# A decoder layer in fp32 parts: the left factors of the fourth unit made early, four raw rooms, and a retuned modulation ring

## The chip, the cores and the metric

The kernel runs on one core of one Trainium2 chip. The metric is the device time of one execution in microseconds, as the median of several runs. The engines are named as in the profile: PE is TensorE (matmuls), PEld its weight loads, DVE is VectorE, ACT is ScalarE, POOL is GpSimd, SP the engine that issues most DMAs.

## The reference, cut to what matters

One decoder layer over 256 tokens of width 2048, all in float32. The layer has a mixer (three attention-like branches behind one wide input projection, joined by `w_out`) and a SwiGLU feed-forward part. Both are modulated by a vector `c`:

```python
mod = jax.nn.silu(c) @ w_ada[l] + b_ada[l]            # 2048 -> 6 x 2048
shift1, scale1, gate1, shift2, scale2, gate2 = jnp.split(mod[:, None, :], N_MOD, axis=-1)
h = rms_norm(x, norm1_gain[l]) * (1 + scale1) + shift1
x = x + gate1 * mixing_sublayer(h, w_in[l], ...)      # ends in y @ w_out
h = rms_norm(x, norm2_gain[l]) * (1 + scale2) + shift2
x = x + gate2 * swiglu(h, w_ffn_in[l], w_ffn_out[l])  # (silu(gate) * up) @ w_ffn_out, width 5632
```

## The kernel before, in words

**Products.** Every float32 weight tile is split into a high and a low part of type float32r: ScalarE casts (`whi`), VectorE subtracts (`wlo`). The left factors (activations, transposed) are split in the same way. `mm3` makes each product from three matmuls: high by high, high by low, low by high (lines 169 to 172). The weights come from HBM in transfers of 512 KB, each into a *raw room*, and are split into a *weight room* (`whi` and `wlo`). In `load_weights` there are four of each. A raw room is free again when the low part has been made; a weight room when TensorE has used it.

**Stages.** The input projection with the three branches; the gates and branch projections (`gate_block`, `y_block`); `w_out` in four column blocks of 512, the last with its weights held for both halves of the tokens; then the eleven units of the feed-forward part, each 512 columns of `gate` and of `up`; then `w_ffn_out` in two output passes of two column blocks each (`fast_products` over `OUT_A`, then over `OUT_B`), the second with a remainder.

**Fast units.** Units 2 to 10 (`FAST`) and both output passes go through `fast_products`. It walks over pairs of 128-row chunks. A *plain* pair is multiplied directly: two column blocks, two halves of the tokens, two chunks, 24 matmuls. A *fast* pair uses seven products in place of eight (Winograd's form of Strassen's scheme), 21 matmuls. For it `load_pair` makes sums and differences of the raw weights on VectorE in two scratch tiles (`ta`, `tb`), and the left factors need sums too. After the last fast pair, four combinations (lines 1427 to 1430) and four additions (`merge`, line 1386) bring the shared products into the four accumulators; the first two additions are wanted by the unit's last pair.

**Left factors of the output passes.** `sums_of_unit(n)` makes the summed and split left factors for one unit of 512 activations, for fast pairs of the output passes. It uses the scratch tiles `AR0` and `A8`, the same that fast pairs of these passes use for `ta` and `tb`. Units 4, 5 and 6 are made at hooks of pairs 2, 4 and 6 of the first pass; the fourth one, unit 3, at the hook of its last pair, with its result in the tiles `OD` and `KD`. Until then `OD` and `KD` serve as two more raw rooms (`more_raws`), so that the first pass has six. Only the second pass uses unit 3's sums.

**Modulation in the background.** The columns of `w_ada` for the later modulations are fetched in steps of 512 KB into a ring of rooms (`ring["tags"]`, two to six of them) and multiplied and added on VectorE (`ada_mac`, line 297). A generator makes one step for each *tick*; each pair of chunks ticks `rate` times, so that a block of 16 chunks makes eight times its rate. `RATES_OP` are the rates of the first three `w_out` blocks, `RATES_FFN` those of the four passes of the first two feed-forward units, whose end flushes what is left; `RATE_OUT` is that of the output passes. `gate2` is made in two portions, 24 steps from the `w_out` stage on and 8 in the first output pass. A multiply-add is written when the ring is full, just before the load that reuses its room, and it is ordered behind the latest weight split of that point (`state["split"]`).

**What sets the order.** All is written once, without loops at run time. A planner puts the instructions of each engine in order: it simulates the program, and when an engine is free, it takes the ready instruction of the highest priority. Priority is program order; `prio()` moves what stands in it `AHEAD` = 4000 instructions forward. A tile with one buffer goes to the next user when the last one lets it go. Weight loads, splits and additions stand in `prio()`; `sums_of_unit` and `ada_mac` do not. On the chip each engine, and SP with its DMAs, goes through its own list in order and waits at each entry for what that entry needs.

Of the kernel before, what the change touches and what calls it, by code (L numbers as in the profile page):

```python
# [31 lines left out]
SEG_SHIFT1, SEG_SCALE1, SEG_GATE1, SEG_SHIFT2, SEG_SCALE2, SEG_GATE2 = range(6)  # L32
RATE_IN, RATE_MID = 0.8, 0.6

RATES_OP, RATES_FFN, RATE_OUT = (0.8, 0.5, 0.15), (0.75, 0.8, 0.6, 0.6), 0.5
GATE2_CUT = 12
LOOK = 3
DEFER = 4
AHEAD = 4000
# [38 lines left out]
def trunk(ctx: ExitStack, tc: tile.TileContext, I, out):  # L78
# [31 lines left out]
    @contextmanager  # L110
    def prio(offset=AHEAD):

        with tc.high_priority(offset=offset):
            start = tc.cur_priority
            yield
            n = tc.cur_priority - start
        tc.cur_priority += n

    state = {"rate": 0.0}
# [239 lines left out]
    ring = {"tags": ("AR0", "AR1"), "n": 0}  # L359
# [5 lines left out]
    macs = []  # L365
# [16 lines left out]
    def ada_segment_steps(acc, seg, done, zero=True, ks=range(KC)):  # L382


        for k in ks:
            for j in range(2):
                while len(macs) >= len(ring["tags"]):
                    mac()
                raw = araw([P, 2 * NB])
                c0 = seg * D + j * 2 * NB  # L390
                with prio():
                    nc.sync.dma_start(raw, w_ada[k * P : (k + 1) * P, c0 : c0 + 2 * NB])
                macs.append((acc, j, k, raw, done if (k, j) == (ks[-1], 1) else None, zero))
                yield
# [976 lines left out]
    def fast_products(src, c0, c1, order, at, sums, own, other, tags, hooks={}, more=False):  # L1371


        ws = []

        def load(n):
            while len(ws) < min(n, len(order)):
                ws.append(load_pair(src, order[len(ws)][0], c0, c1, order[len(ws)][1], tags))

        load(LOOK if hooks else len(order))  # L1380
        o = [[own([P, NB]) for _ in range(NT)] for _ in range(2)]
        shared = []
        end = len(order)
        first_fast, last_fast = (f(n for n, (_, fast) in enumerate(order) if fast) for f in (min, max))
        last_plain = max(n for n in range(last_fast) if not order[n][1])
        add = lambda dst, x: nc.vector.tensor_tensor(dst, dst, x, op=ALU.add)  # L1386

        def merge(half):
            with prio():
                add(o[0][half], (first, third)[half])  # L1390
                add(o[1][half], u[:, 1 - half])

        for n, (p, fast) in enumerate(order):
            tick(2 * state["rate"])
            if n in hooks:
                hooks[n]()
            load(n + LOOK)
            w = ws[n]
            if n == 1 and later:
                with tc.issue_after(state["mm"].ins), prio():  # L1400
                    later.pop()()
            for half in range(2):
                if n == last_fast + 2 + half:
                    merge(half)
            merged = n > last_fast
            if fast:
                if not shared:
                    shared = [other([P, NB]) for _ in range(4)]
                    p1, p5, p7, p6 = shared
                s = sums[p]  # L1410
                a, b = 2 * p, 2 * p + 1
                lefts = (at(a, 0), at(b, 0), s[3], s[0], s[2], s[1], at(b, 1))
                for dst, (h, l), (wh, wl) in zip((p1, o[0][0], o[1][0], p5, p7, p6, o[0][1]), lefts, w):
                    mm3(dst, h, l, wh, wl, n == first_fast and any(dst is x for x in shared), n == last_fast)
            else:
                for c in range(2):
                    for t in range(NT):
                        for k in range(2):
                            h, l = at(2 * p + k, t)

                            closed = n == end - 1 and not more or merged or (c, t) == (1, 1) and n == last_plain
                            mm3(o[c][t], h, l, *w[c][k], n == 0 and k == 0, k == 1 and closed, merged)
            if n == last_fast:
                with prio():
                    u, first, third = S("KC", [P, 2, NB]), S("T6", [P, NB]), scr([P, NB])
                    nc.scalar.copy(first, p1)
                    nc.vector.tensor_tensor(u[:, 0], p6, first, op=ALU.add)
                    nc.vector.tensor_tensor(u[:, 1], p5, u[:, 0], op=ALU.add)
                    nc.vector.tensor_tensor(third, p7, u[:, 0], op=ALU.add)
                    nc.vector.tensor_tensor(u[:, 0], p5, third, op=ALU.add)  # L1430
        for half in range(2):
            if end <= last_fast + 2 + half:
                merge(half)
        return o
# [76 lines left out]
    def sums_of_unit(n):  # L1511

        e = OUT_UNITS[n]
        full = S(OUT_TAGS[0], [P, 4, T])
        nc.vector.tensor_tensor(full, act[e][0].bitcast(F32), act[e][1].bitcast(F32), op=ALU.add)
        sf = S(OUT_TAGS[1], [P, 4, 2, P])
        sums_of(sf, [full[:, :, t * P : (t + 1) * P] for t in range(NT)], slice(0, 4, 2), slice(1, 4, 2))
        hi, lo = (S(tag, [P, 4, 2, P], F32R) for tag in (("H2", "H3"), ("H4", "H5"), ("H6", "H7"), ("OD", "KD"))[n])
        nc.scalar.copy(hi, sf)
        nc.vector.tensor_tensor(lo, sf, hi.bitcast(F32), op=ALU.subtract)  # L1520
        for m in range(2):
            out_sums[2 * e + m] = [(hi[:, j, m, :], lo[:, j, m, :]) for j in range(4)]


    state["more_rooms"] = ()
    state["more_raws"] = ("OD", "KD")
    state["chain"] = None
    hooks = {at: (lambda n=n: sums_of_unit(n)) for n, at in enumerate((2, 4, 6))}
    state["rate"] = RATE_OUT
    ring["tags"] = ("OS1", "OS2")  # L1530
    bg.append(gate2_end())
# [9 lines left out]
    def rows_of_gate2(j):  # L1541
        for c in (slice(0, NB), slice(NB, 2 * NB)):
            ps = misc_bank([P, NB])
            with tc.issue_after(state["mm"].ins):
                for i, x in enumerate(parts[j]):
                    nc.tensor.matmul(ps, ones_r, x[:, c], start=i == 0, stop=i == 1)
            nc.scalar.copy(state["gate2"][j][:, c], ps)
# [7 lines left out]
    behind = 1 + max(n for n, (_, fast) in enumerate(OUT_A) if fast)  # L1555
    assert behind + 2 < len(OUT_A)
    hooks[behind] = lambda: parts_of_gate2(0)
    hooks[behind + 1] = lambda: both(0)
    hooks[behind + 2] = lambda: (rows_of_gate2(1), sums_of_unit(3))
    o = fast_products(w_fo, 0, NB, OUT_A, act_at, out_sums, acc_bank, misc_bank, OUT_TAGS, hooks)  # L1560
    gate2 = [a[:, c : c + NB] for a in state["gate2"] for c in (0, NB)]
    with prio():
        for n in range(2):
            for t in range(NT):
                add_out(n, t, o[n][t])
    state["more_raws"] = ()
    o = fast_products(w_fo, 2 * NB, 3 * NB, OUT_B, act_at, out_sums, misc_bank, acc_bank, OUT_TAGS, more=True)
    for n in (2, 3):
        bring_back(n, f"H{n}")
# [6 lines left out]
    n, pss = 3, o[1]  # L1576
# [42 lines left out]
```

## Time and profile before

| | before |
|---|---|
| median of 3 runs | 1586.41 us (1585.59 to 1587.01) |
| profiled execution, its own time | 1587.38 us |
| its span, first to last instruction | 1585.6 us |
| busy: PE, PEld | 1572.5 us, 1299.3 us |
| busy: DVE, ACT, POOL | 1347.2 us, 860.8 us, 12.4 us |
| moved by DMA | 402.26 MB, mean 254 GB/s |
| granted TensorE clock | 1.000 |

The profile is of one execution, so a time taken from it stands against 1587.38 us, and a median against 1586.41 us. A busy PE is not PE at its peak, because matmuls are pipelined and their ends are modelled; the time between the starts of matmuls, and the busy time of the weight loads in a stretch of fixed length, tell more.

### The profile page before, as it was taken

Reading aid. Unit: us, or ns where it says so; the run is one execution under the profiler, and the core shown is the slowest. Engines: PE = TensorE matmul, PEld = TensorE weight load, DVE = VectorE, ACT = ScalarE, POOL = GpSimd, SP = SyncE. Lnnn points to the kernel's source line nnn. Section 1 sums busy time; section 2 is a strip of 40 time slices with the busy share of each in tenths; the row PEclk is TensorE's granted clock in tenths of the full one; section 3 lists DMA queues with packets and bytes.
Section 4 is the critical chain, followed back from the end, with each engine's and each line's share of the span. In section 5 each row is a group of like instructions: output and inputs, shape, how many; then the busy total and the mean of one; then the engine's idle time right before and its main releaser. Section 6 shows DMA issues by size and latency. Waiting matters only on the chain.

```text
span 1585.6 us, 20226 instructions
## 1 busy us (share of the span) xinstructions
PE 1572.5 (99%) x7219; PEld 1299.3 (82%) x7219; DVE 1347.2 (85%) x1642; ACT 860.8 (54%) x1198; POOL 12.4 (1%) x24
## 2 busy tenths in 40 slices
PE   8999999999999999999999999999999999999998
PEld 7878888888888878888887888888888888888887
DVE  6889996888888686977877887999999998999986
ACT  5654448875765444444444645555555555455553
POOL 1000000000000000000000000000000000000000
PEclk9999999999999999999999999999999999999999
DMA  9999997677788889988888685666666666876664
GB/s 328 361 325 322 335 302 240 222 226 230 230 269 270 302 299 311 318 277 298 293 276 301 210 282 188 212 205 194 199 200 206 196 197 226 290 238 192 223 209 147
DMA packets 196316, 402.26 MB, mean 254 GB/s; under 512 B 13102, under 2 KB 28116, under 8 KB 196216
## 3 DMA queue, kind: packets, MB, share of 16 engines
q1 hardware_dynamic: 194952, 397.75, 76.2%
q0 software_dynamic: 1088, 3.16, 0.5%
q8 instruction: 57, 0.93, 0.2%
q14 instruction: 43, 0.35, 0.1%
q10 hardware_dynamic: 176, 0.07, 0.0%
HBM read 395.68 MB, written 5.24 MB: 253 GB/s over the span
## 4 chain that ended last, share of the span: by engine, by line
PE 88%; DVE 4%; DMA 3%; ACT 3%; issue 2%; POOL 0%; SPq 0%; ACTq 0%; DVEq 0%; POOLq 0%
PE acc L172 21%; PE acc L171 21%; PE acc L170 21%; PE misc L171 6%; PE misc L170 6%; PE misc L172 6%; ACT whi L162 1%; DVE wlo L163 1%; DMA raw<-w_br_gla 1%; PE acc L451 1%; PE misc L820 1%; DMA raw<-w_out 1%; PE misc L1130 1%; DVE wlo L1338 1%; PE misc L444 0%
## 5 line engine op out<-in xcount | busy, mean ns | idle before, releaser
L162 ACT CAST whi<-raw 128x1024 fp32r<-128x1024 f32 x325 | 329.4, 1018 | 352.6 <-PE acc L172 226.6
L163 DVE TENSOR_TENSOR wlo<-raw,whi 128x1024 fp32r<-128x1024 f32 x325 | 380.2, 1178 | 146.5 <-ACT whi L162 144.4
L170 PE MATMUL acc<-whi,H 128*128 128x512 f32 x1145 | 447.3, 392 | 1.1 <-ACT H L463 0.8
L171 PE MATMUL acc<-wlo,H 128*128 128x512 f32 x1145 | 446.9, 390 | 0.8 <-DVE wlo L163 0.7
L172 PE MATMUL acc<-whi,H 128*128 128x512 f32 x1145 | 446.4, 390 | 0.4 <-DVE H L470 0.4
L170 PEld LDWEIGHTS acc<-whi,H 128*128 128x128 f32 x1145 | 214.9, 188 | 45.7 <-ACT H L463 1.3
L172 PEld LDWEIGHTS acc<-whi,H 128*128 128x128 f32 x1145 | 214.8, 188 | 45.8 <-DVE H L470 1.6
L171 PEld LDWEIGHTS acc<-wlo,H 128*128 128x128 f32 x1145 | 215.1, 188 | 44.8 <-DVE wlo L163 1.7
L1352 ACT CAST whi<-raw 128x1024 fp32r<-128x1024 f32 (+1 forms) x163 | 155.4, 968 | 111.8 <-PE acc L172 35.1
L1338 DVE TENSOR_TENSOR wlo<-raw,whi 128x1024 fp32r<-128x1024 f32 (+1 forms) x163 | 177.9, 1114 | 11.1 <-ACT whi L1352 9.8
L172 PE MATMUL acc<-whi,A 128*128 128x512 f32 x234 | 91.1, 390 | 0.0
L171 PE MATMUL acc<-wlo,A 128*128 128x512 f32 x224 | 87.4, 390 | 1.2 <-DVE wlo L163 1.2
L170 PE MATMUL acc<-whi,A 128*128 128x512 f32 x224 | 87.9, 392 | 0.0
L170 PE MATMUL misc<-whi,H 128*128 128x512 f32 (+1 forms) x201 | 78.2, 389 | 0.9 <-DVE misc L1386 0.9
L171 PE MATMUL misc<-wlo,H 128*128 128x512 f32 (+1 forms) x201 | 78.1, 389 | 0.0
L172 PE MATMUL misc<-whi,H 128*128 128x512 f32 (+1 forms) x201 | 77.8, 387 | 0.0
L1338 DVE TENSOR_TENSOR A<-raw,A 128x1024 fp32r<-128x1024 f32 (+2 forms) x59 | 61.2, 1048 | 4.6 <-ACT A L1352 4.2
L1352 ACT CAST A<-raw 128x1024 fp32r<-128x1024 f32 (+1 forms) x47 | 45.9, 989 | 33.4 <-PE acc L172 11.6
L297 DVE SCALAR_TENSOR_TENSOR ada<-AR,csil,ada 128x1024 f32<-128x1024 f32 x39 | 49.4, 1278 | 3.4 <-DMA AR<-w_ada 3.4
L172 PEld LDWEIGHTS acc<-whi,A 128*128 128x128 f32 x234 | 43.9, 188 | 9.1
L171 PEld LDWEIGHTS acc<-wlo,A 128*128 128x128 f32 x224 | 42.1, 188 | 10.4 <-DVE wlo L163 1.9
L170 PEld LDWEIGHTS acc<-whi,A 128*128 128x128 f32 x224 | 42.1, 188 | 9.0 <-ACT whi L162 0.5
(502 smaller groups left out, 2494.7 us busy)
## 6 DMA issues: line engine op xcount, KB each, us to landing
raw<-w_in SPq DMA_DIRECT2D x205, 512.0 KB, 5.1
raw<-w_ffn_in SPq DMA_DIRECT2D x176, 512.0 KB, 4.6
raw<-w_ffn_out SPq DMA_DIRECT2D x74, 512.0 KB, 5.1
AR<-w_ada SPq DMA_DIRECT2D x58, 512.0 KB, 5.0
raw<-w_out SPq DMA_DIRECT2D x32, 512.0 KB, 5.5
OS<-w_ada SPq DMA_DIRECT2D x24, 512.0 KB, 6.1
KC<-w_ada SPq DMA_DIRECT2D x24, 512.0 KB, 5.4
KD<-w_ada SPq DMA_DIRECT2D x21, 512.0 KB, 5.4
```

What stands on the lines that cost most here:

```text
L162: state["cast"] = nc.scalar.copy(hi[:, :n, :], raw[:, :n, :])
L163: state["split"] = nc.vector.tensor_tensor(lo[:, :n, :], raw[:, :n, :], hi[:, :n, :].bitcast(F32), op=ALU.subtract)
L170: nc.tensor.matmul(ps, lh, rh, start=start, stop=False, skip_group_check=seeded)
L171: nc.tensor.matmul(ps, lh, rl, start=False, stop=False, skip_group_check=seeded)
L172: state["mm"] = nc.tensor.matmul(ps, ll, rh, start=False, stop=stop, skip_group_check=seeded)
L297: nc.vector.scalar_tensor_tensor(acc, raw, c, acc, op0=ALU.mult, op1=ALU.add)
L451: state["warm"] = nc.tensor.matmul(ps, ones_r, wide, start=True, stop=True)
L820: nc.tensor.matmul(ps[:n, t * N_GLA + h, :].rearrange("p (s l) -> p s l", l=L), at(f, h, t)[:, :n], odd(at(f, h, t)), start=True, stop=True,)
L1130: nc.tensor.transpose(ps[:, i, :], src[:, i * P : (i + 1) * P], ident)
L1338: done = nc.vector.tensor_tensor(dst, x, y, op=ALU.subtract)
L1352: nc.scalar.copy(hi[:, :n, :], src)
```

## The change

- The rates of the background steps: fewer in the second and third `w_out` blocks, more in two passes of the first two feed-forward units.
- The ring: where it has more than three rooms, a multiply-add is written one step earlier, so that its room is given up a step before the load that reuses it is written.
- The combinations and additions of a unit (`soon`): in the feed-forward units they are moved 8000 instructions forward instead of 4000. The two output passes keep 4000.
- `sums_of_unit(3)` moves from the last pair of the first output pass to pair 8.
- `OD` and `KD` are no raw rooms any more, so the first output pass has four, as the second one has.

```diff
-RATES_OP, RATES_FFN, RATE_OUT = (0.8, 0.5, 0.15), (0.75, 0.8, 0.6, 0.6), 0.5
+RATES_OP, RATES_FFN, RATE_OUT = (0.8, 0.3, 0.0), (0.75, 0.9, 0.7, 0.6), 0.5
...
-                while len(macs) >= len(ring["tags"]):
+                while len(macs) >= len(ring["tags"]) - (len(ring["tags"]) > 3):
                     mac()
...
+        soon = AHEAD if hooks or more else 2 * AHEAD
         load(LOOK if hooks else len(order))
...
         def merge(half):
-            with prio():
+            with prio(soon):
                 add(o[0][half], (first, third)[half])
                 add(o[1][half], u[:, 1 - half])
...
             if n == last_fast:
-                with prio():
+                with prio(soon):
                     u, first, third = S("KC", [P, 2, NB]), S("T6", [P, NB]), scr([P, NB])
...
     state["more_rooms"] = ()
-    state["more_raws"] = ("OD", "KD")
     state["chain"] = None
-    hooks = {at: (lambda n=n: sums_of_unit(n)) for n, at in enumerate((2, 4, 6))}
+    hooks = {at: (lambda n=n: sums_of_unit(n)) for n, at in enumerate((2, 4, 6, 8))}
...
-    hooks[behind + 2] = lambda: (rows_of_gate2(1), sums_of_unit(3))
+    hooks[behind + 2] = lambda: rows_of_gate2(1)
     o = fast_products(w_fo, 0, NB, OUT_A, act_at, out_sums, acc_bank, misc_bank, OUT_TAGS, hooks)
...
-    state["more_raws"] = ()
     o = fast_products(w_fo, 2 * NB, 3 * NB, OUT_B, act_at, out_sums, misc_bank, acc_bank, OUT_TAGS, more=True)
```

## The prediction

> **What bounds the kernel now.** I read the page first, then the stretches of 20 us, then the chain of waits, and last the engines' timelines around each stretch that falls short.
>
> ```profile
> span 1585.6 us, 20226 instructions
> PE 1572.5 (99%) x7219; PEld 1299.3 (82%) x7219; DVE 1347.2 (85%) x1642; ACT 860.8 (54%) x1198; POOL 12.4 (1%) x24
> ```
>
> TensorE is the bound. The profiled execution took 1587.38 us, 1.8 us more than its span and 0.97 us more than the median of 1586.41. No edit removes a matmul, so the change can only win what TensorE now waits, or add waits.
>
> ```profile
> 560.00:580.00 20.00, 19.19 (x84) 15.35 (x83) 15.37 (x17) 7.36 (x7) 0.00 (x0) 1.00 0.87 300
> 840.00:860.00 20.00, 19.44 (x84) 15.12 (x83) 18.11 (x18) 9.57 (x12) 0.53 (x1) 1.00 0.88 291
> 1340.00:1360.00 20.00, 19.08 (x89) 15.56 (x88) 18.48 (x26) 10.95 (x13) 0.00 (x0) 1.00 0.95 347
> 1460.00:1480.00 20.00, 19.70 (x87) 15.61 (x85) 19.57 (x28) 10.41 (x14) 0.00 (x0) 1.00 0.51 169
> 1500.00:1520.00 20.00, 20.00 (x90) 16.57 (x89) 17.60 (x21) 11.23 (x12) 0.00 (x0) 1.00 0.77 239
> 960.00:1300.00 340.00, 340.00 (x1533) 282.15 (x1533) 315.11 (x381) 192.08 (x215) 0.09 (x1) 1.00 0.63 200
> ```
>
> After each stretch and its length stand the busy times of TensorE, its weight loads, VectorE, ScalarE and GpSimd with their counts, the granted clock, the DMA share and GB/s. A full stretch holds 16.57 us of weight loads (1500:1520), so what is missing measures the loss: (16.57-15.35)/16.57x20 = 1.5 us in the first row, 1.75 in the second, 1.2 in the third. In the fourth, part of what is missing is smaller matmuls, so I measure it by starts below. The granted clock is 1.00 throughout. The 340 us of fast units lose nothing. Hence the stock that this change can draw on is about 5 us, of which the stretch at 560 lies in a stage that only the ring edit reaches.
>
> ```profile
> 575.00 0.50 PE L171 MATMUL acc<-wlo,A 128*128 128x512 f32 x1 [0.76 <-DVE wlo L163]
> 853.29 0.39 PE L170 MATMUL acc<-whi,A 128*128 128x512 f32 x1
> 854.09 0.50 PE L171 MATMUL acc<-wlo,A 128*128 128x512 f32 x1 [0.41 <-DVE wlo L163]
> 1340.62 0.39 PE L170 MATMUL misc<-whi,H 128*128 128x512 f32 x1
> 1340.85 0.39 PE L171 MATMUL misc<-wlo,H 128*128 128x512 f32 x1
> ...
> 1343.11 0.39 PE L172 MATMUL misc<-whi,H 128*128 128x512 f32 x1
> 1344.42 0.47 PE L170 MATMUL misc<-whi,H 128*128 128x512 f32 x1 [0.92 <-DVE misc L1386]
> 1479.09 0.61 PE L170 MATMUL acc<-whi,H 128*128 128x512 f32 x2
> 1480.00 0.50 PE L170 MATMUL acc<-whi,H 128*128 128x512 f32 x1 [0.30 <-ACT whi L1352]
> ```
>
> Matmuls of 512 columns start 0.23 us apart (1340.62, 1340.85). From 1343.11 to 1344.42 is 1.31, a stall of 1.1. The pair at 1479.09 puts its second start at 1479.32; to 1480.00 is 0.68, a stall of 0.45, and with the slower restart about 0.55. The waits named are the additions (L1386), a cast and twice a split.
>
> **Part 1, additions of the fast units at twice the priority.**
>
> ```profile
> 1334.44 3.49 DVE L1338 TENSOR_TENSOR wlo<-raw,whi 128x1024 fp32r<-128x1024 f32 x3
> 1337.85 0.68 DVE L1427 TENSOR_TENSOR KC<-acc,T 128x512 f32<-128x512 f32 x1
> ...
> 1341.84 1.23 DVE L1338 TENSOR_TENSOR wlo<-raw,whi 128x1024 fp32r<-128x1024 f32 x1 [1.52 <-ACT whi L1352]
> 1342.98 0.69 DVE L1430 TENSOR_TENSOR KC<-acc,scr 128x512 f32<-128x512 f32 x1
> 1343.58 0.69 DVE L1386 TENSOR_TENSOR misc<-misc,KC 128x512 f32<-128x512 f32 x1
> 1340.76 1.05 ACT L1352 CAST whi<-raw 128x1024 fp32r<-128x1024 f32 x1 [4.29 <-DMA raw<-w_ffn_out]
> ```
>
> In the last fast unit the first combination (L1427) sits behind three splits of 1.16, and the last one (L1430) behind a split whose cast waited 4.29 us for the first weights of the output pass. VectorE then stands idle 1.52 us although L1430's input is ready. With the doubled offset the four combinations and first two additions (6 x 0.60 to 0.69 = 3.9) go ahead of at least two of the three splits: they run from about 1335.6 and end about 1339.5, where TensorE wants the last of them at 1343.34. The 1.1 us go, with the slow restart 1.2. Late next are the displaced splits: the second would end at 1340.8, just when TensorE reads it (1340.85), so up to 0.3 could come back. The other eight fast units have the same code, but the 340 us row shows no loss there; the split that the additions can overtake belongs to the unit's last pair, which TensorE reads some 5 us later. I book 0, with a bound of 0.6 for one late split. Total -1.2 (from -1.2 to +0.6; not lower, as no more is lost there).
>
> **Part 2, the fourth unit's left factors moved from the last pair of the first output pass to its pair 8.**
>
> ```profile
> 1471.47 1.22 DVE L1515 TENSOR_TENSOR AR<-A,A 128x1024 f32<-128x1024 f32 x1
> 1472.72 0.76 DVE L1306 TENSOR_TENSOR A<-AR 128x256 f32<-128x256 f32 x2
> 1473.85 0.42 DVE L1306 TENSOR_TENSOR A<-AR,A 128x256 f32<-128x256 f32 x1
> 1476.12 1.22 DVE L1520 TENSOR_TENSOR KD<-A,OD 128x1024 fp32r<-128x1024 f32 x1
> 1474.31 1.05 ACT L1519 CAST OD<-A 128x1024 fp32r<-128x1024 f32 x1 [1.87 <-DVE A L1306]
> 1478.90 1.05 ACT L1352 CAST whi<-A 128x1024 fp32r<-128x1024 f32 x1 [2.13 <-DVE A L1338]
> ```
>
> Removed here: 1.22, four short sums from 1472.72 to 1474.27 (1.55) and 1.22, together 4.0 us of VectorE, and 1.05 of ScalarE, all right before the first fast pair of the second output pass, which needs the same scratch tiles AR0 and A8. The cast at 1478.90 waited 2.13 us for that pair's last difference, and TensorE at 1480.00 waits for the cast. Without the 4.0 us the 0.55 stall goes. No DMA moves with it. It is added where three sister units already run without a stall, ahead of their hook because their inputs are long there; VectorE stands idle in that place:
>
> ```profile
> 1376.70 1.23 DVE L1338 TENSOR_TENSOR wlo<-raw,whi 128x1024 fp32r<-128x1024 f32 x1 [1.22 <-ACT whi L1352]
> ```
>
> Splits there wait for casts, and casts for TensorE to free a weight room, so VectorE has such gaps, and a plain pair lets a split be some 5 us late; the 4.0 fit in. If instead the planner lets pair 8 take AR0 and A8 first, the 4.0 and the cast's 1.05 stand before pair 10, which needs the same tiles and whose splits are wanted at once, and TensorE could lose as much: +5.1 at most. I take 0, by the three sisters. Total -0.55 (from -0.55 to +4.5).
>
> **Part 3, four raw rooms instead of six in the first output pass.** Per plain pair TensorE works 24 x 0.227 = 5.44 us on two transfers of 512 KB, so four rooms turn over in 10.9 us. A turn costs the landing, a cast (1.05) and a split (1.23).
>
> ```profile
> raw<-w_ffn_out SPq DMA_DIRECT2D x74, 512.0 KB, 5.1
> DMA to landing us min/median/max: 4.5/7.4/10.0
> ```
>
> The first row is the page's median over all. The second is the raw tiles' own answer for 1331 to 1345, when six loads, two of gate2 and two of the modulation are in flight together. By the first a turn is 7.4, by the worst 12.3. The second output pass is the same loop with four rooms and loses nothing (1500:1520), so I book 0; fewer loads in flight at 1335 even help. Bounds 0 and, below as a rival, +15.
> [...]
>
> **Part 4, rates.** A block of 16 chunks ticks eight times. In the first three `w_out` blocks the steps fall from 8x(0.8+0.5+0.15) = 11.6 to 8x(0.8+0.3) = 8.8; in the first two FFN units they rise from 22 to 23.6, and 15 instead of 12 steps fall there.
>
> ```profile
> 840.81 1.28 DVE L297 SCALAR_TENSOR_TENSOR T<-A,csil,T 128x1024 f32<-128x1024 f32 x1
> ...
> 849.59 1.27 DVE L297 SCALAR_TENSOR_TENSOR T<-A,csil,T 128x1024 f32<-128x1024 f32 x1
> 844.44 2.71 SPq L148 DMA_DIRECT2D raw<-w_out  x2
> 850.77 1.05 ACT L162 CAST T<-raw 128x1024 fp32r<-128x1024 f32 x1 [3.02 <-DMA raw<-w_out]
> 852.81 1.23 DVE L163 TENSOR_TENSOR wlo<-raw,whi 128x1024 fp32r<-128x1024 f32 x1 [1.34 <-ACT whi L162]
> 900.00:960.00 60.00, 60.00 (x270) 49.80 (x269) 45.88 (x42) 26.58 (x28) 0.98 (x2) 1.00 0.78 251
> ```
>
> Five multiply-adds stand from 840.81 to 849.59, with their transfers between the weights of the last `w_out` block, where TensorE eats 512 KB per 1.36 us. The load issued at 844.44 lands 6.3 us later; its cast at 850.77 holds the next cast and so the split at 852.81 and TensorE at 854.09. With the new rates three remain, and one transfer fewer (512 KB at 291 GB/s, 1.8 us) stands before or beside that load. The first two multiply-adds, which delay SP's 844.44, may stay, so the gain lies between 0 and 1.75. I take -1.0: one transfer of 1.8 is more than the 0.6 of the first stall, less than the whole. The three steps cost 3 x 1.28 = 3.8 us of VectorE in the FFN, covered by 14 idle us in 900:960; three transfers more lift a DMA share of 0.78 by 0.09. Bounds -1.75 and +0.5.
>
> **Part 5, the ring.** With more than three rooms a multiply-add is written one step earlier than the load that reuses its room. Nothing is added; one room lies empty a step longer.
>
> ```profile
> 555.93 2.66 SPq L392 DMA_DIRECT2D AR<-w_ada  x2
> 559.87 0.39 SPq L148 DMA_DIRECT2D raw<-w_br_gla  x1
> ```
>
> SP issues in order, and at 555.93 to 559.87 a weight load stands behind modulation loads that wait for multiply-adds; its late landing makes the stall at 575.00. A step's lead can shorten this, or only shift the burst by a step. Bounds -1.5, the whole loss of the stretch at 560, and +1.5, the same once more; I take -0.3, nearer to the shift.
>
> **Sum.** -1.2 -0.55 +0 -1.0 -0.3 = -3.05: 1584.3 for a profiled execution like this one, 1583.4 as a median.
>
> **Rivals.**
> (a) The ring also closes the stall at 575: -1.5 in place of -0.3, total -4.25, 1582.2. For it speaks the SP row; against it that the multiply-adds of a block still come in one burst.
> (b) An edit does not do what it says: the planner still finds the first `w_out` loads late, or sets L1430 behind a split again because its input is not yet written when VectorE falls free. Then only one of parts 1 and 4 counts, with part 2: -1.55 to -1.75, 1584.8.
> (c) Slower: four rooms are too few while the first pass also carries modulation loads. It decides from a landing of 10.9-1.05-1.23 = 8.6 us; at 10.0 each turn of four loads loses 1.4, so eight plain pairs (four turns) lose 5.6 and all 22 pairs (eleven turns) 15. The total is +2.5 to +12, 1589 to 1598. For it: the 10.0 above, and the modulation loads. Against it: the second pass, and that those 10.0 came from ten loads in flight.
>
> **How the numbers follow.** A measurement of this kernel can tell about 0.2%, 3.2 us, from no change: below 1583.2 is faster, up to 1589.6 the same. The forecast (-2.5 to -3.9) gets 0.42, half of it on either side of the 3.2; (a) 0.24, faster; (b) 0.14, same; (c) and part 2's bad order 0.20, put as slower. So faster 0.45, same 0.35, slower 0.20. The range goes from -5.0, all four stalls gone in full, to +3.4, (c) just past the first eight pairs, each widened by the 0.7 by which the runs shown scatter (1585.59 to 1587.01): 1580.7 to 1590.5. It leaves out the worse part of (c). The side of fewer waits alone is 1580.7 to 1584.8.
>
> **What would show it.** Right: no start later than 0.5 us after its forerunner near 1343 and 1480; L1430 next to L1429; L1515 four times before 1385; `w_out` stretch above 16 us of weight loads. Wrong: repeated casts "<-DMA raw<-w_ffn_out" with TensorE gaps between 1350 and 1445 (part 3), a gap near 1404 (part 2), new gaps in 960 to 1300 (part 1), or in 860 to 960 (part 4).

## The result

| | before | after |
|---|---|---|
| median | 1586.63 us (1585.51 to 1589.33, 16 runs) | 1589.91 us (1587.93 to 1595.06, 16 runs) |
| ratio to before | 1 | 1.0022, 95% interval 1.0015 to 1.0029 |
| profiled execution, its own time | 1587.38 us | 1589.98 us |
| its span | 1585.6 us | 1588.2 us |

The change makes the kernel slower by 3.3 us. The forecast was 1583.4 us, so the sign was wrong; the measured time lies inside the stated range, near its upper end (1590.5). Three of the stalls of before (575, 1344 and 1480) are gone, and one that the prediction had named and booked at nothing, near 1404, came in their place.

### The profile page after: what moved, and what is told of

The parts are those of the page before. It is cut to its first block, busy times and chain, and to the rows that moved or that the text cites. A ratio compares the mean times of both kernels' runs of the same rounds, so it can differ in the third digit from the quotient of the medians.

```text
span 1588.2 us, 20218 instructions
## 1 busy us (share of the span) xinstructions
PE 1573.6 (99%) x7219; PEld 1300.6 (82%) x7219; DVE 1348.2 (85%) x1642; ACT 861.3 (54%) x1198; POOL 12.8 (1%) x24
## 4 chain that ended last, share of the span: by engine, by line
PE 86%; DVE 5%; DMA 5%; issue 2%; ACT 2%; SPq 0%; ACTq 0%; DVEq 0%
PE acc L172 21%; PE acc L171 21%; PE acc L170 21%; PE misc L171 6%; PE misc L172 6%; PE misc L170 6%; DMA raw<-w_ffn_in 2%; DVE wlo L163 2%; DVE wlo L1339 1%; DMA raw<-w_in 1%; PE acc L452 1%; PE misc L821 1%; DMA AR<-w_ada 1%; ACT whi L162 1%; PE misc L1131 0%
## 5 line engine op out<-in xcount | busy, mean ns | idle before, releaser
L1353 ACT CAST whi<-raw 128x1024 fp32r<-128x1024 f32 (+1 forms) x177 | 169.0, 970 | 120.1 <-PE acc L172 41.2
L1339 DVE TENSOR_TENSOR wlo<-raw,whi 128x1024 fp32r<-128x1024 f32 (+1 forms) x177 | 193.5, 1117 | 13.2 <-ACT whi L1353 11.8
L1339 DVE TENSOR_TENSOR A<-raw,A 128x1024 fp32r<-128x1024 f32 (+2 forms) x61 | 62.6, 1037 | 6.0 <-ACT A L1353 5.5
L1353 ACT CAST A<-raw 128x1024 fp32r<-128x1024 f32 (+1 forms) x47 | 45.9, 988 | 35.1 <-DMA raw<-w_ffn_in 12.6
L297 DVE SCALAR_TENSOR_TENSOR ada<-AR,csil,ada 128x1024 f32<-128x1024 f32 x39 | 49.7, 1280 | 2.3 <-DMA AR<-w_ada 2.0
```

What stands on the lines that cost most here:

```text
L297: nc.vector.scalar_tensor_tensor(acc, raw, c, acc, op0=ALU.mult, op1=ALU.add)
L1339: done = nc.vector.tensor_tensor(dst, x, y, op=ALU.subtract)
L1353: nc.scalar.copy(hi[:, :n, :], src)
```

## The profile after

In the kernel after, lines behind the edits have other numbers: L1515 has become L1518 (first sum of `sums_of_unit`), L1306 L1307, L1519 L1522, L1520 L1523, L1338 and L1352 (split and cast) L1339 and L1353, L1386 (additions) L1389, L1427 to L1430 L1430 to L1433.

The first view is again the busy times by stretch, with the same columns and the same six stretches as before:

```profile
560.00:580.00 20.00, 20.00 (x90) 16.57 (x89) 17.22 (x18) 7.38 (x7) 0.00 (x0) 1.00 0.94 331
840.00:860.00 20.00, 19.36 (x85) 15.68 (x84) 14.96 (x16) 9.43 (x12) 0.53 (x1) 1.00 0.85 277
1340.00:1360.00 20.00, 20.00 (x94) 16.65 (x93) 19.97 (x27) 11.46 (x13) 0.00 (x0) 1.00 0.88 315
1460.00:1480.00 20.00, 19.84 (x88) 15.77 (x87) 18.73 (x24) 9.54 (x12) 0.00 (x0) 1.00 0.66 213
1500.00:1520.00 20.00, 20.00 (x90) 16.57 (x89) 17.61 (x20) 11.56 (x12) 0.00 (x0) 1.00 0.79 258
960.00:1300.00 340.00, 339.74 (x1531) 281.68 (x1530) 316.19 (x381) 192.21 (x215) 0.53 (x1) 1.00 0.63 201
```

The weight loads of the first stretch rose from 15.35 to the full 16.57, those of the third from 15.56 to 16.65. The second rose from 15.12 to 15.68 only. The last row lost 0.5 us of weight loads, too little to account for the loss. That stands in a stretch that was full before; its two halves, before and then after:

```profile
1400.00:1405.00 5.00, 5.00 (x23) 4.00 (x22) 4.94 (x7) 2.89 (x3) 0.00 (x0) 1.00 0.86 238
1405.00:1410.00 5.00, 5.00 (x23) 4.12 (x23) 5.00 (x6) 2.69 (x4) 0.00 (x0) 1.00 0.86 302
```

```profile
1400.00:1405.00 5.00, 3.33 (x15) 2.15 (x13) 4.90 (x8) 2.43 (x3) 0.00 (x0) 1.00 0.31 112
1405.00:1410.00 5.00, 4.22 (x13) 3.36 (x14) 4.75 (x5) 3.67 (x4) 0.00 (x0) 0.72 0.78 227
```

Before, the two held 23 matmuls each; after, 15 and 13. VectorE is busy nearly throughout in both kernels (4.90 of 5 us after), and in the second half after the granted clock is 0.72. TensorE's own rows, after:

```profile
1402.38 0.40 PE L172 MATMUL acc<-whi,H 128*128 128x512 f32 x1
1402.61 0.72 PE L170 MATMUL misc<-whi,H 128*128 128x512 f32 x2
1405.78 0.50 PE L170 MATMUL misc<-whi,H 128*128 128x512 f32 x1 [2.45 <-ACT whi L1353]
1406.11 0.40 PE L171 MATMUL misc<-wlo,H 128*128 128x512 f32 x1
...
1407.31 0.63 PE L171 MATMUL misc<-wlo,H 128*128 128x512 f32 x1
1407.74 0.63 PE L172 MATMUL misc<-whi,H 128*128 128x512 f32 x1
1408.16 0.63 PE L171 MATMUL acc<-wlo,A 128*128 128x512 f32 x1
```

TensorE stands idle 2.45 us until a cast, then seven matmuls follow each other at 0.427 instead of 0.227 us. With the start-to-start time above 0.227 us as measure, the stall costs 2.6 us and the slow matmuls behind it 1.8, together about 4.4. Summed over the program (neighbouring matmuls of 512 columns, without the first 10 us) this excess is 15.1 us before and 17.5 after.

Why the cast is late stands in VectorE's rows and in that of the cast on ScalarE, after:

```profile
1388.84 1.23 DVE L1339 TENSOR_TENSOR wlo<-AR,whi 128x1024 fp32r<-128x1024 f32 x1 [1.12 <-ACT whi L1353]
1390.10 1.23 DVE L1518 TENSOR_TENSOR AR<-A,A 128x1024 f32<-128x1024 f32 x1
1391.57 1.23 DVE L1339 TENSOR_TENSOR wlo<-A,whi 128x1024 fp32r<-128x1024 f32 x1 [0.24 <-ACT whi L1353]
1392.71 1.28 DVE L297 SCALAR_TENSOR_TENSOR A<-OS,csil,A 128x1024 f32<-128x1024 f32 x1
1393.90 3.49 DVE L1339 TENSOR_TENSOR wlo<-raw,whi 128x1024 fp32r<-128x1024 f32 x3
1397.31 1.28 DVE L297 SCALAR_TENSOR_TENSOR A<-OS,csil,A 128x1024 f32<-128x1024 f32 x1
1398.51 0.75 DVE L1307 TENSOR_TENSOR A<-AR 128x256 f32<-128x256 f32 x2
...
1400.09 0.69 DVE L1339 TENSOR_TENSOR AR<-raw,raw 128x512 f32<-128x512 f32 x1
...
1401.90 1.22 DVE L1523 TENSOR_TENSOR KD<-A,OD 128x1024 fp32r<-128x1024 f32 x1
1403.15 0.69 DVE L1339 TENSOR_TENSOR A<-raw,AR 128x512 f32<-128x512 f32 x1
1403.88 0.69 DVE L1339 TENSOR_TENSOR A<-raw,A 128x512 f32<-128x512 f32 x1
1404.68 1.04 ACT L1353 CAST whi<-A 128x1024 fp32r<-128x1024 f32 x1 [2.13 <-DVE A L1339]
```

`AR0` and `A8` have one buffer each and go from hand to hand in program order: pair 8, unit 3's sums, pair 10. Pair 8, the first fast pair of the pass, lets AR0 go at 1390.1 and A8 at 1392.8. The sums take AR0 at once, but their short sums (L1307) come only at 1398.51, behind three splits and two multiply-adds; L1523 reads A8 until 1403.1. Only then can pair 10 write A8, and its cast runs from 1404.68 to 1405.72. VectorE splits pair 10's AR0 behind these differences, so that low part ends at the same moment (1405.71). The place in program order is in the code: a pair's load is written two pairs ahead of its products, behind the hook (`LOOK` = 3). So what hook 8 writes comes behind pair 8's load and ahead of pair 10's.

In the kernel before, with a multiply-add between pair 10's two last differences:

```profile
1402.37 0.68 DVE L1338 TENSOR_TENSOR A<-OD,A 128x512 f32<-128x512 f32 x1
1403.80 0.39 PE L172 MATMUL acc<-whi,H 128*128 128x512 f32 x1
```

The second row is the matmul that starts at 1402.38 in the kernel after, which is 1.4 us ahead at this place. Against TensorE's stream, pair 10's last difference therefore comes 2.9 us later than before, not 1.5.

Two more new stalls, both smaller. The second norm, after, on VectorE and then on TensorE:

```profile
881.13 0.21 DVE L270 SCALAR_TENSOR_TENSOR tiny<-tiny,tiny 128x1 f32<-128x1 f32 x1
881.26 1.28 DVE L297 SCALAR_TENSOR_TENSOR T<-A,csil,T 128x1024 f32<-128x1024 f32 x1
882.45 0.15 DVE L271 TENSOR_SCALAR tiny<-tiny 128x1 f32<-128x1 f32 x1
```

```profile
885.34 0.40 PE L172 MATMUL acc<-T,H 128*128 128x512 f32 x1
886.35 0.50 PE L170 MATMUL acc<-whi,H 128*128 128x512 f32 x1 [0.61 <-ACT H L1221]
```

A multiply-add (L297) has slipped between two small steps of the norm, which lengthens a chain that nothing hides; TensorE's excess at 880 to 900 rises from 0.17 to 1.24 us. Before, L271 followed L270 directly. The other, 0.4 us at 979, is in the profiles of only one of the five experiments that share this kernel's order of instructions up to 1357, so it belongs to the execution rather than to the change.

## Experiments

Each was timed in turns with the kernel before on the same chip, in groups on different chips; so the ratios compare better than the medians (that of before alone is 1586.35 to 1586.95 us from group to group). "Excess at 1405" is the sum of what the start-to-start times have above 0.227 us between 1400 and 1420, from each one's profiled execution; "none" is under 0.25 us, 0.1 before.

| kernel | median us | ratio to before (95%) | excess at 1405 |
|---|---|---|---|
| after | 1589.91 | 1.0022 (1.0015 to 1.0029) | 4.5 |
| after, factors at the last pair | 1587.23 | 1.0005 (0.9997 to 1.0014) | none |
| after, factors at pair 6 | 1586.67 | 1.0001 (0.9992 to 1.0010) | none |
| after, own scratch tiles | 1587.38 | 1.0002 (0.9993 to 1.0011) | none |
| after, factors at pair 10 | 1591.05 | 1.0029 (1.0017 to 1.0040) | 4.0 |
| after, sums in `prio()` | 1588.79 | 1.0012 (1.0003 to 1.0020) | 2.6 |
| before + additions | 1586.18 | 0.9996 (0.9987 to 1.0005) | none |
| before + rates | 1586.12 | 0.9999 (0.9990 to 1.0008) | none |
| before + ring | 1587.03 | 1.0007 (0.9998 to 1.0016) | none |
| before + four rooms | 1587.45 | 1.0005 (0.9996 to 1.0014) | 0.5 |
| before + four rooms and factors at pair 8 | 1589.64 | 1.0020 (1.0010 to 1.0030) | 4.3 |
| before + additions, four rooms, factors at pair 6 | 1587.35 | 1.0005 (0.9996 to 1.0014) | none |
| after, factors at pair 6, ring lead early only | 1586.25 | 0.9995 (0.9986 to 1.0004) | none |

**Is it the place of the left factors?** In the kernel after, they go back to the last pair; everything else of the change stays, the four rooms too.

```diff
-    hooks = {at: (lambda n=n: sums_of_unit(n)) for n, at in enumerate((2, 4, 6, 8))}
+    hooks = {at: (lambda n=n: sums_of_unit(n)) for n, at in enumerate((2, 4, 6))}
...
-    hooks[behind + 2] = lambda: rows_of_gate2(1)
+    hooks[behind + 2] = lambda: (rows_of_gate2(1), sums_of_unit(3))
```

> The changed kernel with the fourth unit's left factors back at the last pair of the first output pass; the four raw rooms, the ring, the rates and the additions stay changed. Theory (scratch tiles): the factors stood between pair 8 and pair 10, which use the same scratch tiles AR0 and A8, so the stall near 1405 of 2.6 us and the slow restart of 1.7 behind it go, and the stall of 0.5 at the beginning of the second output pass comes back: about 1589.9 - 4.4 + 0.5 = 1586.0. Rival (rooms): four raw rooms starve the first pass, so a stall stays near 1405 or moves a little, about 1589 to 1590.

1587.23 us and no stall at 1405: 2.7 us less than after, from this one edit, though 1.2 us above the forecast. The stall at the start of the second pass is back (excess 0.75 in 1460 to 1500, as before), and a new one of 1.38 us at 1456 shows what four rooms can cost: SP issues four loads in a row, a cast waits for one of them, the split of that cast waits in turn, and TensorE waits for an addition (L1389) that stands behind the split. It is the pattern that part 1 removed from the feed-forward units; the output passes keep the 4000. No run tried 8000 there.

```profile
1444.92 3.77 SPq L1333 DMA_DIRECT2D raw<-w_ffn_out  x4
```

```profile
1453.04 1.05 ACT L1353 CAST whi<-raw 128x1024 fp32r<-128x1024 f32 x1 [3.05 <-DMA raw<-w_ffn_out]
1456.01 0.50 PE L170 MATMUL acc<-whi,H 128*128 128x512 f32 x1 [1.22 <-DVE acc L1389]
```

**Is it the order of the tiles, or just being early?** Now the factors are made even earlier, at pair 6 behind the third unit's.

```diff
-    hooks = {at: (lambda n=n: sums_of_unit(n)) for n, at in enumerate((2, 4, 6, 8))}
+    hooks = {at: (lambda n=n: sums_of_unit(n)) for n, at in enumerate((2, 4, 6))}
+    hooks[6] = lambda: (sums_of_unit(2), sums_of_unit(3))
```

> The changed kernel with the fourth unit's left factors written at the hook of pair 6, right behind the third unit's, so that they get AR0 and A8 before pair 8 does; the same work, only its turn at the two tiles differs. Theory (scratch tiles): the stall near 1405 and the slow clock behind it go, nothing comes back, about 1589.9 - 4.4 = 1585.5. Rival (VectorE has no room for 4 us more in the first pass): the stall stays, only earlier, 1588 to 1590. Rival (rooms): it stays near 1405.

1586.67 us, 3.2 us less than after, though 1.2 us above the forecast. The same instructions now have the two tiles before the first fast pair wants them; from the timeline of VectorE, with the factors at pair 6:

```profile
1373.66 0.75 DVE L1307 TENSOR_TENSOR A<-AR 128x256 f32<-128x256 f32 x2
...
1377.46 1.22 DVE L1523 TENSOR_TENSOR KD<-A,OD 128x1024 fp32r<-128x1024 f32 x1
```

They end at 1378.7, and pair 8 begins at 1383.8. The stretch of 1460 to 1480 in the same kernel shows that what part 2 was to win is really there, once the place is right:

```profile
1460.00:1480.00 20.00, 20.00 (x89) 16.38 (x89) 17.09 (x22) 10.64 (x13) 0.00 (x0) 1.00 0.57 190
```

**Is it the tiles or the 4 us of work?** The factors stay at pair 8 but use two other scratch tiles, so that they need not wait for pair 8 nor pair 10 for them.

```diff
-        full = S(OUT_TAGS[0], [P, 4, T])
+        full = S(OUT_TAGS[0] if n < 3 else "KD", [P, 4, T])
...
-        sf = S(OUT_TAGS[1], [P, 4, 2, P])
+        sf = S(OUT_TAGS[1] if n < 3 else "KC", [P, 4, 2, P])
```

> The changed kernel with the fourth unit's left factors still at pair 8, but in the scratch tiles KC and KD, which no weight pair of this pass uses. Theory (scratch tiles): pair 10 no longer waits for them, the stall near 1405 falls from 4.3 us in all to under 0.5, about 1585.5 to 1586. Rival (VectorE's own time): the 4 us of work still stand in a stretch where VectorE is busy throughout, so a stall of 2 us and more stays, 1588 and above.

1587.38 us, and the stretch at 1405 is full again, 45 matmuls in 10 us against 28 in after; from the stretches of this kernel:

```profile
1400.00:1410.00 10.00, 10.00 (x45) 8.05 (x44) 9.85 (x12) 5.37 (x7) 0.00 (x0) 1.00 0.84 282
1440.00:1460.00 20.00, 18.33 (x81) 14.67 (x80) 15.77 (x19) 10.14 (x11) 0.00 (x0) 1.00 0.65 208
```

So the tiles were what lacked. With tiles of their own the sums no longer wait for pair 8 and end at 1379.7, ahead of it, where VectorE has the time: behind them it is idle for 0.52 us before 1381.32 and for 0.30 before 1384.04. Whether it would have had time for them between pair 8 and pair 10, this run does not show: no sums stand there any more. The second row is the same stall at the end of the pass as above, 2.1 us in this execution.

**Does the stall follow the place?** The factors two pairs later, at pair 10.

```diff
-    hooks = {at: (lambda n=n: sums_of_unit(n)) for n, at in enumerate((2, 4, 6, 8))}
+    hooks = {at: (lambda n=n: sums_of_unit(n)) for n, at in enumerate((2, 4, 6, 10))}
```

> The changed kernel with the fourth unit's left factors at pair 10 in place of 8, so between the fast pairs 10 and 12. Theory (scratch tiles): the stall moves with them by one fast and one plain pair, 10.2 us, to about 1415, and is again 2.5 to 4.5 us with its restart; total 1588.5 to 1590.5. Rival (rooms, or the last modulation loads and the residual fetched back near 1400): the stall stays near 1405.

It does: 1591.05 us, a little more than forecast (its profile also has 2.2 us at the end of the pass), and in TensorE's timeline the stall stands 11 us later, with the same length and the same releaser, and a shorter one ahead of it:

```profile
1413.28 0.50 PE L171 MATMUL acc<-wlo,H 128*128 128x512 f32 x1 [0.72 <-DVE wlo L1339]
1417.02 0.50 PE L170 MATMUL misc<-whi,H 128*128 128x512 f32 x1 [2.46 <-ACT whi L1353]
```

**Is low priority to blame?** The sums do not stand in `prio()`, and splits overtook them. Here they are put into it.

```diff
-    hooks = {at: (lambda n=n: sums_of_unit(n)) for n, at in enumerate((2, 4, 6, 8))}
+    hooks = {at: (lambda n=n: sums_of_unit(n)) for n, at in enumerate((2, 4, 6))}
+
+    def fourth():
+        with prio():
+            sums_of_unit(3)
+    hooks[8] = fourth
```

> The kernel after, with the fourth unit's left factors still made at pair 8, but inside prio(), so that they are ordered 4000 instructions forward, like the splits. Rival, the low priority: the sums are late only because splits and multiply-adds go ahead of them; then with the priority they run straight behind pair 8's last difference, pair 10 gets AR0 and A8 in time, the stall near 1405 (2.6 us and 1.7 us of slow restart) falls below 1 us and the time comes to that of the version with the factors at pair 6, about 1586.7. Theory, the turn of the two tiles: the sums still stand between pair 8 and pair 10, and no order of theirs shortens their own 4.0 us of VectorE and 1.05 us of ScalarE; A8 is let go by pair 8 at about 1392.8, casts to raw weights, splits and sums run from there, and pair 10's last difference comes no earlier than about 1402 against 1403.9. Then at least 2 us of the 4.3 us stay, and the time stays at 1589 to 1591. I hold the theory likelier, 0.7.

1588.79 us: between the two theories, nearer to that of the tiles. This profile is 0.8 us ahead of that of after where pair 8 ends (its split of AR0 begins at 1388.01 instead of 1388.84). With that taken off, the short sums begin 2.3 us earlier (at 1395.34 instead of 1398.51), but pair 10's last difference only 0.4 us earlier (1402.69 instead of 1403.88), since the sums themselves still stand before it; TensorE's timeline has two stalls left:

```profile
1402.10 0.50 PE L171 MATMUL acc<-wlo,H 128*128 128x512 f32 x1 [0.67 <-DVE wlo L1339]
...
1404.58 0.50 PE L170 MATMUL misc<-whi,H 128*128 128x512 f32 x1 [1.19 <-ACT whi L1353]
```

In sum 2.2 us, and no slow matmuls behind them. By these two profiles, sums held between pair 8 and pair 10 cost 2.2 even with priority; the low priority adds 0.4 of wait, and 1.8 of slow clock in the one execution profiled (the slow clock does not follow every such stall, see the last section). The intervals of the two ratios, 1.0012 and 1.0022, overlap a little.

**The five parts alone, on the kernel before.** First the additions (`soon`), the rates and the ring, each by itself, with the lines of the diff shown above.

> The kernel before with the additions of the feed-forward units at the doubled offset and nothing else. Theory (each part does what it says, the scratch tiles alone turned the sign): the stall of 1.2 us at 1344 goes and no other moves, 1586.4 - 1.2 = 1585.2. Rival: the gap at 1344 is closed in the changed kernel only because the output pass no longer loads into OD and KD, so that here the stall stays, 1586.4.

1586.18 us. The stall at 1344 is gone (16.64 us of weight loads in 1340 to 1360), but the time falls by a ratio of 0.9996 that cannot be told from none.

> The kernel before with the changed rates alone. Theory: they shorten the stall of 1.4 us near 854, and bring the new one of 0.9 to 1.2 us near 886, where the first feed-forward unit takes up more background steps; together -0.5 to +0.5, 1586 to 1587. Rival: the stall at 886 belongs to the ring, so here 854 shortens and 886 stays clean, 1585.5.

1586.12 us. The `w_out` stretch holds 15.24 us of weight loads, against 15.12 before; four multiply-adds stand in it instead of five. No stall at 886.

> The kernel before with the changed ring alone. Theory: the earlier multiply-add lets the weight loads of the first branch product through, the stall of 1.35 us at 575 goes, 1585.0. Rival: the ring also makes the stall near 886, then 1586.2.

1587.03 us. The stall at 575 is gone, and the one at 886 has come; from the stretches of the kernel with the ring alone:

```profile
560.00:580.00 20.00, 20.00 (x90) 16.53 (x90) 18.05 (x19) 8.81 (x9) 0.00 (x0) 1.00 0.96 335
880.00:890.00 10.00, 9.38 (x50) 7.49 (x48) 9.45 (x19) 5.16 (x14) 0.53 (x1) 1.00 0.93 328
```

Then the rooms, alone and together with the factors at pair 8.

```diff
-    state["more_raws"] = ("OD", "KD")
...
-    state["more_raws"] = ()
```

> The kernel before with four raw rooms in the first output pass and nothing else; the fourth unit's factors stay at the last pair. Theory: four rooms are enough for most of the pass, but its last pairs, where the next pass begins to load, get their weights late: a stall of 0.4 to 1.8 us near 1457 as in the kernels with the factors moved back, and none between 1350 and 1445; 1586.4 to 1588. Rival (four rooms cost nothing): no gap there, 1586.4.

1587.45 us. The pass is not starved (an excess of 0.5 us at 1400 to 1420). The stall expected near 1457 is not in this profile (0.17 us in 1440 to 1460). The stall at 1344 goes here too, without the additions' priority. SP issues four loads of the pass between 1336 and 1340, where before there were six between 1332 and 1339; that this is the reason is argued, not tested.

```diff
-    state["more_raws"] = ("OD", "KD")
-    hooks = {at: (lambda n=n: sums_of_unit(n)) for n, at in enumerate((2, 4, 6))}
+    hooks = {at: (lambda n=n: sums_of_unit(n)) for n, at in enumerate((2, 4, 6, 8))}
...
-    hooks[behind + 2] = lambda: (rows_of_gate2(1), sums_of_unit(3))
+    hooks[behind + 2] = lambda: rows_of_gate2(1)
...
-    state["more_raws"] = ()
```

> The kernel before with only the fourth unit's left factors at pair 8 and, since they need OD and KD, four raw rooms; rates, ring and additions are as before. Theory: this alone turns the sign. A stall of 2 to 3 us of which TensorE's first cast of pair 10 is the end near 1404, then some eight matmuls at about 0.43 us apart with a granted clock of about 0.57 in those 4 us; in sum 4 to 4.5 us, less 0.5 near 1480, and so 1589.5 to 1591 as a median, ratio 1.002 to 1.003. Rival, that the other edits are needed too (the additions at doubled priority or the ring shift the splits so that pair 10 comes late): no stall over 1 us between 1400 and 1410, and 1586.5 to 1587.5, as with four rooms alone.

1589.64 us, the whole loss with none of the other edits. TensorE's timeline of it:

```profile
1404.12 0.80 PE L170 MATMUL misc<-whi,H 128*128 128x512 f32 x1 [2.45 <-ACT whi L1352]
1404.71 0.63 PE L171 MATMUL misc<-wlo,H 128*128 128x512 f32 x1
```

The ratios less 1 of additions, rates, ring, and rooms with factors, -0.0004, -0.0001, +0.0007 and +0.0020, add up to +0.0022, what the whole change shows; each has an uncertainty of about 0.0009, so the close agreement is partly luck.

**A better version?** First the parts that looked good, without ring and rates: before with `soon`, four rooms and both third and fourth unit at `hooks[6]`.

> A version put together from what the runs showed: the kernel before with the additions at doubled priority, four raw rooms and the fourth unit's left factors at pair 6, right behind the third unit's, and with the ring and the rates of before. Theory: the stalls at 1344 (1.2 us) and 1480 (0.55 us) are gone, none comes at 1405 and none at 886 (1.24 us, which came with the ring); the one at 575 (about 1 us) stays, and the end of the first pass may cost 0.7 us. That makes -1.2 -0.55 +0.7 = -1.05 us: 1585.5, ratio 0.9993. Rival, that such sums of single stalls don't add up because loads that start earlier come due at other places: 1586.5 to 1587.5, no different from before, with new stalls of 0.5 to 2 us somewhere else.

1587.35 us, no better than before. No stall at 1344, 1405, 1480 or 886, but 1.8 us more of excess than in the profile of before at 860 to 880, and 0.6 at the end of the pass. The rival's time came, but not by its cause: up to 1331 the instructions of TensorE, VectorE, ScalarE and SP stand in the same order as before, so loads that start earlier cannot have made the stall at 860.

Then the kernel after with the factors at pair 6 and the ring's lead only in the gate and branch stage.

```diff
-                while len(macs) >= len(ring["tags"]) - (len(ring["tags"]) > 3):
+                while len(macs) >= len(ring["tags"]) - (ring["tags"][0] == "AR0" and len(ring["tags"]) > 3):
...
-    hooks = {at: (lambda n=n: sums_of_unit(n)) for n, at in enumerate((2, 4, 6, 8))}
+    hooks = {at: (lambda n=n: sums_of_unit(n)) for n, at in enumerate((2, 4, 6))}
+    hooks[6] = lambda: (sums_of_unit(2), sums_of_unit(3))
```

> The kernel after with the fourth unit's left factors at pair 6 behind the third unit's, and with the ring's lead only in the gate and branch stage (the rings that begin with AR0), not in the w_out and feed-forward stages. Theory: the lead closes the stall at 575 because SP no longer waits for multiply-adds there, and it opens the one at 886 because it lets a multiply-add of 1.28 us (L297) fall between two small steps of the second norm (L270 and L271). Here both stalls are gone, so that the profile shows no gap over 0.3 us near 575, 886, 1344, 1405 and 1480, and the excess of starts is about 11.5 us against 12.7 with the factors at pair 6 alone and 15.1 in the kernel before; the median comes to about 1585.3, ratio 0.999. Rival: the 886 stall has another cause (the rates, which bring other steps there), and stays at 1.2 us; then 1586.5 as with the factors at pair 6. Whether either is told from the kernel before is open, since single stalls move by 1 to 2 us between executions.

The cause of the stall at 886 is confirmed: L271 follows L270 again, and the stretch is full. From the stretches of this version:

```profile
560.00:580.00 20.00, 20.00 (x90) 16.58 (x89) 17.20 (x19) 7.38 (x7) 0.00 (x0) 1.00 0.94 328
880.00:890.00 10.00, 10.00 (x53) 8.17 (x52) 9.39 (x25) 7.41 (x17) 0.00 (x0) 1.00 0.53 175
1340.00:1360.00 20.00, 20.00 (x94) 16.61 (x93) 19.96 (x27) 11.64 (x14) 0.00 (x0) 1.00 0.89 319
1400.00:1410.00 10.00, 10.00 (x46) 8.08 (x45) 9.94 (x12) 5.58 (x6) 0.00 (x0) 1.00 0.80 265
```

The excess is 11.9 us and the span 1582.3, the shortest of all. Its median is 1586.25 us, a ratio of 0.9995 (0.9986 to 1.0004): clearly below after's 1.0022, and not to be told from before. The profiled execution, 1584.2 us, is one of the fastest of its eleven.

## Why the prediction was wrong

**The step that failed is in part 2: "I take 0, by the three sisters."** The bound beside it had the mechanism, its place and nearly its size: pair 8 takes AR0 and A8 first, then 4.0 and 1.05 us stand before pair 10, up to +5.1 at the gap near 1404. The trace shows 4.4 us at 1405.78. What chose wrongly between the ends of the bound was the comparison with the sister units. Their hooks, pairs 2, 4 and 6, all stand before the first fast pair of the pass, so nobody else wanted the tiles, and the sums ran ahead of their hook. `OUT_A` in the code makes pair 8 that first fast pair, so the fourth unit's sums were the only ones to come between two users of the tiles. That could be read before the run. The row that was quoted for the cover, VectorE idle for 1.22 us at 1375, was right but lay where the sisters run. Where the tiles held the fourth unit's sums, from pair 8's split of AR0 to pair 10's first difference, VectorE of the kernel before is idle for 1.5 us, less than the 4.0 it had to take up. With own tiles the same work at the same hook ran before pair 8 and cost nothing at 1405.

That the measured time lies in the range is luck: its upper end was set by rival (c), too few rooms, which did not happen.

**Part 2's gain** of 0.55 us is real: in after, no stall is left at the start of the second pass (the excess in 1480 to 1500 falls from 0.57 to none). The stall is in none of the eight profiles with the factors moved forward and in all six of the others. Part 2's total was +3.9 instead of -0.55.

**Part 1** did in the profile what was written, -1.2 of excess at 1344, with the combinations and additions between 1335.9 and 1340.7. The three profiles with neither this edit nor four rooms (before, rates, ring) have 0.8 to 1.3 us there, the others none, so 1.2 is at the upper end. Alone its ratio is 0.9996, and the interval holds 1.

**Part 3**, booked at 0, was right inside the pass: between 1350 and 1445 three casts of after wait 2.7 us in all for weights, and TensorE loses nothing by it. Its end costs 0 to 2.2 us in different versions and executions; the four profiles with six rooms show nothing there. Rival (c) had the right cause for that and the wrong place and size. The measured time fell inside its 1589 to 1598, but for part 2's reason.

**Part 4** was mis-sized. Three multiply-adds instead of five stand there in after, but with the rates alone four; the count came out only together with the ring's lead. The excess in 840 to 860 fell from 1.43 to 0.95 and by 0.1 with the rates alone, not by 1.0. Even the 0.5 lies inside the scatter: 1.0 to 1.5 in the five profiles with before's order there, 0.95 to 1.3 in the six with after's. The first stall at `w_out` stays, 0.8 us at 853 behind a split, with two transfers of the modulation fewer; what makes it late stays open.

**Part 5** was booked at -0.3, nearer to "a shift". The closed stall at 575 was -1.35 against the profile of before, as in rival (a), and the multiply-add in the second norm +1.1. The six profiles with the old ring have 0.2 to 1.4 us at 575, 0.8 on average, so the gain is more like 0.8. The net is small, but not for the reason given: the lead did bring two weight loads forward, issued at 562.40 in after instead of 564.72 (SP's waits for multiply-adds between 540 and 580 still add up to 12.0 us, against 12.1), and the price appeared in another stage, where the range had no row for it. The sign named for it, a gap in 860 to 960, was put down to part 4.

Set against the profile of before in stretches of 20 us, the excess of after changes by -1.4 (575), -0.5 (`w_out`), +1.1 (886), +0.5 (979), -1.2 (1344), +4.4 (1405), +0.45 (the end of the first pass) and -0.6 (1480): +2.75 in all. The whole excess rose by 2.4 and the profiled time by 2.60; the remainder is spread over the other stretches. Single stalls differ by up to 2 us from one profiled execution to the next. In the five profiles with before's order of instructions up to 1331, the stretch at 860 to 880 has 0.5 us twice and 2.3 to 2.4 three times; in the eight with after's order up to 800, the stretch at 400 has 0.2 to 0.3 seven times and 2.4 once, in that of the ring alone. So one profile cannot size a stall to better than that, and differences of this kind would hide the gain of a version with fewer stalls.

## What to carry to other kernels

When work is moved to another place, compare it with its neighbours by what they hold, not only by what they cost: list who has each one-buffer tile just before and just after the new place. Here, work of low priority that takes such a tile keeps it until it has had its turn, and everything of high priority behind it inherits that priority. And a lead given to a background step moves it in every stage that uses the same ring: look for serial chains of small steps there, where a single instruction of 1.28 us has no cover.

## What the hardware showed

The stall was made longer by the clock. These are stretches of the kernel after, cut at the matmuls that are slow:

```profile
1405.50:1407.20 1.70, 1.42 (x6) 1.20 (x7) 1.65 (x3) 1.70 (x3) 0.00 (x0) 1.00 0.80 198
1407.20:1410.40 3.20, 3.20 (x10) 2.47 (x9) 3.00 (x3) 1.47 (x2) 0.00 (x0) 0.50 0.83 262
1410.40:1415.00 4.60, 4.60 (x21) 3.79 (x20) 4.60 (x8) 1.67 (x2) 0.00 (x0) 0.98 0.66 212
```

The trace's own clock entries have it at 0.50 from 1407.21 to 1410.62, for 3.4 us, and that begins 1.4 us after TensorE has started again. With four rooms and the factors at pair 8 alone it is 0.50 from 1403.78 to 1407.19, again 3.4 us, and that begins 0.3 us before the restart at 1404.12. In the profile with the factors at pair 10 a stall of the same length (2.85 us from start to start in all three) is followed by no slow matmul. Stalls of 1.3 to 2.1 us from start to start (575 and 1344 before, 1458 with own tiles, 1404.58 with the sums in `prio()`) were not followed by one either, nor was one of 2.35 at 400 with the ring alone.

A long stall is not the only occasion. Two of the fourteen profiles, those of the ring alone and of before with additions, four rooms and factors at pair 6, show the halved clock near the start as well, for 3.4 us; with the ring alone:

```profile
33.59:37.00 3.41, 3.41 (x9) 2.63 (x8) 3.12 (x9) 1.54 (x2) 0.00 (x0) 0.50 0.91 296
```

Just before it, from 30.5 to 32.6, TensorE has only eight matmuls of one column and two of 128, and then 0.8 us of idle time. All fourteen kernels have the same instructions in the same order there, and in the profile of before the clock is 1.00 from 33.59 to 37.00, after the same 0.80 us of idle time; so the program alone does not decide whether the clock is halved.

The mean clock of each execution, rounded to 0.001, gives an estimate of how often it happens, though not where: 3.4 us at 0.50 in a span of 1588 take off 0.001, and the four profiled executions with a halved stretch above are all at 0.999 (so are those of the additions alone and of the rates alone). It is below 1.000 in 24 of the 30 executions of the three kernels with the stall of 2.85 us (after, four rooms and factors at pair 8, factors at pair 10), and in 2 of the 44 of the versions of after without a stall at 1405; but also in 30 of the 102 of before, whose stalls are shorter. The three executions of after at 1.000 took 1587.93 to 1589.62 us, so the stall costs time without the slow clock too.

Of three stalls with nearly the same idle time, 2.45 us (after), 2.45 (four rooms and factors at pair 8) and 2.46 (factors at pair 10), the halved clock came with the first two and not with the third. What decides it, there and at the start of the program, is not shown: no run here varied that alone.
